# A two-layer backbone in one kernel: another order of block products in the first MLP, one chain for the plain blocks, and modulation rows in another place

## The chip, the cores and the metric

The kernel runs on one core of one Trainium2 chip, as one program. The metric is the device time of one execution in microseconds; the median of several executions counts. A core has TensorE (PE, the matmuls), VectorE (DVE), ScalarE (ACT), GpSimd (POOL) and SyncE (SP), which here only issues DMA loads. ACT and POOL issue the stores. Each engine works through its own instructions in order and waits for others by semaphores. Matmul results lie in PSUM until another engine moves them out.

## What is computed

Two layers over 1024 latent and 256 context tokens of width 1024. Each has a modulated in-projection, a mix of differential attention, a short convolution and a Fourier transform, an out-projection with gated residual and layer norm, and an MLP with squared ReLU and again gated residual and norm:

```python
for l in range(DEPTH):                                  # 2
    mod_x = (silu_c @ w_mod[l] + b_mod[l])[:, None, :]  # six rows of 1024; the same for the context
    sh1, sc1, g1, sh2, sc2, g2 = jnp.split(mod_x, 6, axis=-1)
    px = modulate(x, sh1, sc1) @ w_in[l]                # x*(1+scale) + shift; also for ctx
    ...                                                 # attention, convolution, Fourier mix -> mix_x
    x = layer_norm(DEEPNORM_ALPHA * x + g1 * mix_x, ln1_g[l], ln1_b[l])
    x = layer_norm(DEEPNORM_ALPHA * x
                   + g2 * (jnp.square(jax.nn.relu(modulate(x, sh2, sc2) @ w_up[l])) @ w_down[l]),
                   ln2_g[l], ln2_b[l])
    if not last: ...                                    # the same two steps for ctx with its own gates
return x
```

Everything is float32. The first layer's MLP works on 1280 tokens (ten tiles of 128), the second layer's end on 1024.

## The kernel before

Each float32 product is made of three matmuls: an operand x is split into hi (a cast on ACT) and lo = x − hi (line 230, on DVE or POOL), and `mm3` issues hi·hi, hi·lo and lo·hi (lines 234 to 236). So each weight and each activation needs an ACT cast and a lo before PE can use it.

**First MLP, up.** The 32 hidden blocks of 128 are 4 plain ones (`plain`, whole products) and 14 pairs (p = 2 to 15). A pair is computed as a 2x2 block product with seven products rather than eight, `mlp_blocks0`. They are named 1, 5, 6, 2, 7, 3, 4; each has 24 matmuls of 320 columns. Products 1, 2 and 5 open a PSUM tile, 6, 7 and 4 go on in that of 1, and 3 in that of 5. So between 6, 7 and 4 the tile's value is copied out, and after 7 DVE reads the tile of 5 too (line 1931) before 3 may go on in it. The list `seq` sets the order of products over pairs, and for product n the work of the other engines is written out behind it: evacuation of n, hi of n+3, lo of n+2, weight sums of n+4, and the step `back` of the background work. `wload(p + 2)` at product 3 loads the weights of the next pair but one.

**First MLP, down.** `down_blocks` is a generator that the up part starts early with `next(down)`. It makes 7 groups of 35 products (6 matmuls of 512 columns each), with operands formed by `form`. Its 8 PSUM tiles are added into ten token tiles `acc[t]` by `evac` (line 2217). The table `tail` loads what comes next during the last products. Then the plain loop multiplies two plain blocks per token tile, adds them, multiplies the tile by the gate on POOL (line 2158, `fold_late`), and adds the residual on DVE (line 2161). `wm` converts weights; for the last tiles they are multiplied with the gate on POOL first (line 2172).

**Finish.** `finish_steps` does the other two plain blocks (`down(t)`, add in line 2397, statistics in 2398 to 2405), the norm (`fin`), the transposes for the next in-projection (`turn`, line 2413), and the first parts of that in-projection (`part`). Line 2405 is a power of −1/2 on POOL, and line 2381 a small product on DVE that needs it; the helper `stats` has the same pair in lines 1267 and 1269.

**In-projection and modulation.** The modulation rows of the second layer are computed on DVE in the background, since each is a vector times a matrix. `mod_jobs` makes 16 jobs per row, each with a load of 256 KB and accumulations (lines 337 and 339), and each four jobs end in a `mod_tail` with small matmuls on PE (lines 383 or 386) and a small DVE step (lines 392 or 399). `in_steps` runs them between its units and works off the rest at its end, before it starts the second V projection (`vproj`, evacuated in lines 604 and 606). `REST` numbers the rows: 6 is gate one of the second layer, 7 its gate two, 8 and 9 shift and scale two. `mlp_blocks` is the second layer's MLP with a similar order of products.

## Time and profile before

| what | value |
| --- | --- |
| median of three executions | 3020.53 us (3015.72 to 3021.08) |
| the profiled execution | 3015.05 us, of it the span 3013.3 us |
| PE busy | 2749.9 us, 91% |
| DVE, ACT, POOL busy | 2068.2, 1153.4, 1127.3 us |
| mean granted clock of TensorE | 0.96 |
| DMA | 469.21 MB, mean 156 GB/s |

The span is the profiled execution from its first to its last instruction, and the rest of its time lies around it. Times in rows count from the span's start. Where the granted clock is below 1.00, part of a stretch ran at 1.2 rather than 2.4 GHz, and PE's busy time there is longer for the same matmuls. A bracket in a timeline row is the time its engine was idle before, and the instruction that ended that. The stages lie in this order: first in-projection, attention and out-projection to about 780, plain blocks and pairs to 1220, down to 1578, plain loop and finish to 1683, second in-projection to 1940, attention and out-projection to 2390, second MLP up to 2650, down and the end to 3013.

### The profile page before, as it was taken

The numbers are of one execution on the slowest core, as the hardware profiler recorded it, in microseconds if no ns is written. First come the engines' busy times: TensorE is split into PE (matmuls) and PEld (weight loads), VectorE is DVE, ScalarE is ACT, GpSimd is POOL, SyncE is SP. The second block draws the span as 40 slices with busy tenths as digits, with TensorE's granted clock in tenths as the row PEclk, the third lists the DMA queues.
The fourth block names the chain that finished last, engine by engine and source line by source line (L and its number), as shares of the span: only waits on it lengthen the run. The fifth ranks groups of instructions, "written<-read, shape, count | busy, mean of one in ns | idle before, by whom it ended". The sixth has DMA issues, their size and how long they took to land. (4 is left out here: it accounts for less than half of the span.)

```text
span 3013.3 us, 37703 instructions
## 1 busy us (share of the span) xinstructions
PE 2749.9 (91%) x14290; PEld 2349.5 (78%) x14290; DVE 2068.2 (69%) x2926; ACT 1153.4 (38%) x1610; POOL 1127.3 (37%) x642
## 2 busy tenths in 40 slices
PE   7889999899889999899996999779989899999996
PEld 5788888778789999787784888668777778878875
DVE  6668778844557777578877565647845577568887
ACT  4221256524434344433321531126623455554331
POOL 3412145623100000465647710126756000048785
PEclk8999999999999999899998999889999999999998
DMA  6244652346545554534351344643346555464442
GB/s 255 81 165 130 199 129 52 121 161 229 192 160 206 173 171 153 215 127 147 121 190 59 112 147 158 201 123 88 112 152 190 180 187 199 154 237 151 150 161 91
DMA packets 229033, 469.21 MB, mean 156 GB/s; under 512 B 18958, under 2 KB 116724, under 8 KB 228852
## 3 DMA queue, kind: packets, MB, share of 16 engines
q1 hardware_dynamic: 208680, 395.43, 40.6%
q10 hardware_dynamic: 17292, 61.93, 5.3%
q0 software_dynamic: 2880, 9.44, 0.8%
q8 instruction: 113, 1.85, 0.2%
q14 instruction: 68, 0.56, 0.1%
HBM read 323.41 MB, written 143.31 MB: 155 GB/s over the span
## 5 line engine op out<-in xcount | busy, mean ns | idle before, releaser
L234 PE MATMUL q<-a,a 128*128 128x512 f32 (+1 forms) x1632 | 599.0, 367 | 53.8 <-DVE t L1931 26.7
L236 PE MATMUL q<-a,a 128*128 128x512 f32 (+2 forms) x1682 | 611.5, 364 | 3.2 <-DVE a L230 3.2
L235 PE MATMUL q<-a,a 128*128 128x512 f32 (+1 forms) x1618 | 591.7, 366 | 5.5 <-POOL a L230 5.5
L235 PE MATMUL p<-a,b 128*128 128x512 f32 (+1 forms) x1088 | 407.1, 374 | 1.1 <-POOL a L230 1.0
L234 PEld LDWEIGHTS q<-a,a 128*128 128x128 f32 x1632 | 311.2, 191 | 107.0 <-DVE t L1931 30.5
L230 POOL TENSOR_TENSOR a<-b,a 128x256 fp32r<-128x256 f32 (+2 forms) x163 | 249.2, 1539 | 331.8 <-ACT a L2081 156.4
L236 PEld LDWEIGHTS q<-a,a 128*128 128x128 f32 x1682 | 320.4, 190 | 47.0 <-DVE a L230 4.7
L235 PEld LDWEIGHTS q<-a,a 128*128 128x128 f32 x1618 | 309.0, 191 | 48.4 <-POOL a L230 6.7
L2217 DVE TENSOR_TENSOR b<-q,b 128x512 f32<-128x512 f32 x425 | 279.2, 684 | 95.7 <-PE q L236 95.2
L230 DVE TENSOR_TENSOR a<-a,a 128x1280 fp32r<-128x1280 f32 (+4 forms) x156 | 290.1, 1860 | 43.2 <-ACT a L2078 31.8
L234 PE MATMUL p<-a,b 128*128 128x512 f32 (+1 forms) x816 | 305.2, 374 | 7.5 <-ACT b L1833 3.6
L236 PE MATMUL p<-a,b 128*128 128x512 f32 (+1 forms) x800 | 293.1, 366 | 3.9 <-DVE b L230 3.9
L234 PE MATMUL q<-b,a 128*128 128x256 f32 (+1 forms) x740 | 255.9, 346 | 41.0 <-DVE b L2217 15.8
L230 POOL TENSOR_TENSOR a<-a,a 128x1024 fp32r<-128x1024 f32 (+2 forms) x49 | 134.0, 2737 | 399.6 <-ACT a L2081 330.5
L339 DVE SCALAR_TENSOR_TENSOR m<-w,k,m 128x256 f32<-128x256 f32 x448 | 228.8, 523 | 48.1 <-DMA w<-wmr 38.8
L236 PE MATMUL q<-b,a 128*128 128x256 f32 (+1 forms) x740 | 252.6, 341 | 0.6 <-DVE a L230 0.6
L235 PE MATMUL q<-b,a 128*128 128x256 f32 (+1 forms) x740 | 252.7, 342 | 0.0
L235 PEld LDWEIGHTS p<-a,b 128*128 128x128 f32 x1088 | 208.2, 191 | 33.9 <-POOL a L230 1.9
L958 DVE TENSOR_REDUCE c<-p 128x1 f32<-128x1280 f32 x128 | 190.6, 1489 | 64.1 <-PE p L956 62.9
L989 ACT ACTIVATE a<-p,c 128x1280 f32<-128x1280 f32 x128 | 170.5, 1332 | 90.0 <-DVE c L958 82.6
L234 PEld LDWEIGHTS q<-b,a 128*128 128x128 f32 x740 | 144.7, 196 | 64.4 <-DVE b L2397 14.6
L234 PEld LDWEIGHTS p<-a,b 128*128 128x128 f32 x816 | 156.2, 191 | 34.3 <-issue 4.7
(300 smaller groups left out, 5412.6 us busy)
## 6 DMA issues: line engine op xcount, KB each, us to landing
a<-d SPq DMA_DIRECT2D x88, 512.0 KB
w<-wmr SPq DMA_DIRECT2D x160, 256.0 KB
a<-d SPq DMA_DIRECT2D x56, 640.0 KB
b<-wu SPq DMA_DIRECT2D x64, 512.0 KB
d<-t SPq DMA_DIRECT2D x46, 640.0 KB
b<-wd SPq DMA_DIRECT2D x54, 512.0 KB
d<-a ACTq DMA_DIRECT2D x40, 640.0 KB
a<-d SPq DMA_DIRECT2D x80, 320.0 KB
```

The source lines that it names most:

```text
L230: (eng or self.nc.vector).tensor_tensor(out, x, hi, op=ALU.subtract)
L234: mm(out, lh, rh, start=start, stop=False, skip_group_check=on)
L235: mm(out, lh, rl, start=False, stop=False, skip_group_check=on)
L236: mm(out, ll, rh, start=False, stop=stop, skip_group_check=on)
L339: nc.vector.scalar_tensor_tensor(a, w[:, i], s, a, op0=ALU.mult, op1=ALU.add)
L958: nc.vector.reduce_max(mx, ps[:, :nkey], axis=AX.X, negate=True)
L989: self.nc.scalar.activation(e[:, :nkey], ps[:, :nkey], AF.Exp, bias=mx, accum_out=s)
L2217: v.tensor_tensor(a, ps, a, op=ALU.add)
```

## The change

1. `in_steps`: the second layer's rows are 6, 8 and 9 rather than 6 to 9. Row 7 is computed in the second layer's MLP, which gets `tail` steps at products 7 and 3, and a `back` step at product 2 too.
2. `stats`: −mean on DVE first, then the power and the product on POOL. `finish_last` and the finish use it.
3. `mlp_blocks0`: another `seq`, the first two weights converted within the last plain block, and `wload(p + 2)` earlier in the step of product 3.
4. `down_blocks` in the first layer: the lo of the first group's weights on DVE, a further `yield`, evacuation after one product, and all four plain weights and activations loaded and converted in `tail`. The plain loop, `fold_late` and the scaling of weights are gone.
5. `finish_steps`: one chain over all four plain blocks per token tile and half (`half`), then `gate` on POOL, `resid` on DVE one tile later, and `norm`. The weights of the in-projection are loaded and converted at t = 8 and after rather than from t = 0.

```diff
@@ in_steps
-        for i in range(NREST0) if l == 0 else range(NREST1, len(REST)):
+        for i in (6, 8, 9) if l else range(NREST0):
@@ stats
+        m = self.sm([128, 1], bufs=12)
+        nc.vector.tensor_scalar(m, mv[:, 0:1], -1.0, None, op0=ALU.mult)
         nc.gpsimd.tensor_tensor(r, r, self.mhalf[:, 0:1], op=ALU.pow)
-        nc.vector.scalar_tensor_tensor(m, mv[:, 0:1], -1.0, r, op0=ALU.mult, op1=ALU.mult)
+        nc.gpsimd.tensor_tensor(m, m, r, op=ALU.mult)
@@ mlp_blocks
-        bg = self.stream(self.resid_jobs(l, T))
+        bg = self.stream(self.resid_jobs(l, T) + self.mod_jobs(7))
-            if i in (5, 6, 4, 3):
+            if i in (5, 6, 2, 4, 3):
                 back()
+            if i in (7, 3):
+                tail()
@@ mlp_blocks0
-        seq = [(NPL, 1), (NPL, 2)]
-        for p in range(NPL, NP):
-            seq += [(p, 5), (p, 6)] + [(p, 2)] * (p > NPL) + [(p, 7), (p, 3)]
-            seq += [(p + 1, 1)] * (p < NP - 1) + [(p, 4)]
+        a, b = NPL, NPL + 1
+        seq = [(a, 1), (a, 2), (b, 1), (a, 5), (a, 6), (b, 2), (a, 7), (a, 3), (a, 4)]
+        seq += [(b, 5), (b, 6), (b + 1, 1), (b, 7), (b, 3), (b, 4)]
+        for p in range(b + 1, NP):
+            seq += [(p, 5), (p, 6), (p, 2), (p, 7)] + [(p + 1, 1)] * (p < NP - 1) + [(p, 3), (p, 4)]
...
-        st.append(plain(3, {0: [P(sum_add, 3)], 1: [P(sum_split, 3), st[2], P(wload, NPL + 1)], 2: [back], 3: [back],
-                            4: [back], 5: [back]}))
+        st.append(plain(3, {0: [P(sum_add, 3)], 1: [P(sum_split, 3), P(wload, NPL + 1), P(wsum, 0), P(wsum, 1)],
+                            2: [lambda: st[2](), back], 3: [back], 4: [P(whi, 0), P(wlo, 0)], 5: [P(whi, 1), P(wlo, 1)]}))
...
+            if i == 3:
+                wload(p + 2)
             wsum(k + 4)
...
-            if i == 3:
-                wload(p + 2)
...
-            if p == NP - 1 and i in (2, 7, 3):
+            if p == NP - 1 and i in (6, 2, 7, 3, 4):
                 next(down)
@@ down_blocks
-            self.lo(wl, x, wh, g)
+            self.lo(wl, x, wh, g if n or l else v)
+        if l == 0:
+            yield
...
-            tail = {-16: P(wl, 0), -13: P(wl, 1), -12: P(wm, False), -10: P(hraw, 0), -9: P(wm, False), -8: P(hraw, 1),
-                    -7: hconv, -6: gload, -5: hconv, -4: P(gload, 1), -3: P(rload, 0), -2: P(rload, 1)}
+            tail = {-20: P(wl, 0), -18: P(wl, 1), -16: whi, -15: wlo, -14: P(wl, 2), -13: whi, -12: wlo,
+                    -11: P(hraw, 0), -10: whi, -9: wlo, -8: hconv, -7: P(hraw, 1), -6: P(wl, 3), -5: hconv,
+                    -4: [P(hraw, 2), P(hraw, 3)], -3: [gload, P(rload, 0)], -2: hconv, -1: whi}
+        lag = 2 if l else 1
-            evac(2, ps)
+            evac(lag, ps)
...
-        for t in range(T):                     # the plain loop: 6 matmuls per tile and half,
-            ...                                # an add each, fold_late(t), the tasks of tile t
+        wlo()
+        hconv()
+        self.gs[1] = self.bcast(self.grow[(l, 5, 1)])
@@ finish_steps
+        def half(t, c):
+            ps = self.p1()
+            sl = slice(128 * t, 128 * t + 128)
+            for i in range(4):
+                self.mm3(ps, H[i][0][:, sl], H[i][1][:, sl], W[i][0][:, c:c + 512], W[i][1][:, c:c + 512], i == 0, i == 3)
+            y = self.acc[t][:, c:c + 512]
+            nc.vector.tensor_tensor(y, ps, y, op=ALU.add)
+        def gate(t):
+            nc.gpsimd.tensor_tensor(y, y, self.gs[int(t >= 8)], op=ALU.mult)
+        def resid(t):
+            nc.vector.scalar_tensor_tensor(y, xr.pop(t)[:, :D], ALPHA, y, op0=ALU.mult, op1=ALU.add)
+        def norm(t):                           # bn_stats of both halves, stats(), Identity on ACT, store
+        def down(t):
+            half(t, 0);   resid(t - 1)
+            half(t, 512); norm(t - 1)
+            gate(t);      rload(t + 1)
```

PE, at the join of products 7 and 3 in the middle of the pairs: before, the last matmul of 7 and the first of 3, then the joins to (p+1, 1) and to 4. `q_1323` is the tile of product 1, `q_1332` that of 5, `q_1347` that of the next pair.

```order
L236 MATMUL q_1323_8121<-t_1232_6797,a_1025_5530 128x320
L234 MATMUL q_1332_8201<-a_1026_5531,a_1018_5523 128x320
...
L236 MATMUL q_1332_8201<-a_1032_5537,a_1019_5524 128x320
L234 MATMUL q_1347_8390<-a_1018_5523,a_1020_5525 128x320
...
L236 MATMUL q_1347_8390<-a_1024_5529,a_1021_5526 128x320
L234 MATMUL q_1323_8121<-a_1203_6652,a_1022_5527 128x320
```

```order
L236 MATMUL q_1322_8091<-t_1232_6807,a_1025_5532 128x320
L234 MATMUL q_1344_8356<-a_1018_5525 128x320
...
L236 MATMUL q_1344_8356<-a_1024_5531,a_1019_5526 128x320
L234 MATMUL q_1331_8205<-a_1026_5533,a_1020_5527 128x320
...
L236 MATMUL q_1331_8205<-a_1032_5539,a_1021_5528 128x320
L234 MATMUL q_1322_8091<-a_1203_6662,a_1022_5529 128x320
```

Product 3 (`q_1332`, now `q_1331`) stood right behind 7 and now stands behind product 1 of the next pair (`q_1344`).

POOL, in the plain loop before and in the finish after: `b` are the token tiles, line 2158 and after it line 2382 the gate, 1269 and 1270 power and product, `c` columns of 128.

```order
L2172 TENSOR_TENSOR a_1814_12865<-a_1814_12865,a_1807_12799 128x1024
L2158 TENSOR_TENSOR b_1527_10585<-b_1527_10585,a_1807_12799 128x1024
L230 TENSOR_TENSOR a_1825_12950<-a_1819_12906,a_1824_12949 128x1280
L2158 TENSOR_TENSOR b_1529_10595<-b_1529_10595,a_1807_12799 128x1024
L2172 TENSOR_TENSOR a_1815_12882<-a_1815_12882,a_1807_12799 128x1024
L2158 TENSOR_TENSOR b_1533_10608<-b_1533_10608,a_1807_12799 128x1024
L2158 TENSOR_TENSOR b_1536_10620<-b_1536_10620,a_1807_12799 128x1024
```

```order
L2382 TENSOR_TENSOR b_1521_10559<-b_1521_10559,a_1817_12849 128x1024
L1269 TENSOR_TENSOR c_1836_12962<-c_1836_12962,k_5_75 128x1
L1270 TENSOR_TENSOR c_1837_12964<-c_1837_12964,c_1836_12962 128x1
L2382 TENSOR_TENSOR b_1524_10569<-b_1524_10569,a_1817_12849 128x1024
L1269 TENSOR_TENSOR c_1844_13008<-c_1844_13008,k_5_75 128x1
L1270 TENSOR_TENSOR c_1845_13010<-c_1845_13010,c_1844_13008 128x1
L2382 TENSOR_TENSOR b_1527_10581<-b_1527_10581,a_1817_12849 128x1024
```

Gates stood among weights' products and lo's of 1280 columns, ahead of all statistics; now power, product and gate alternate tile by tile.

DVE, in the finish at one token tile: before the add, statistics and the small product of line 2381 (of the tile before); after the add (2378), the residual (2386) and the statistics.

```order
L2397 TENSOR_TENSOR b_1525_10568<-q_1853_13129,b_1525_10568 128x512
L2398 BN_STATS c_1852_13128<-b_1525_10568 128x6
L2381 SCALAR_TENSOR_TENSOR c_1854_13138<-c_1849_13120,c_1850_13122 128x1
L2397 TENSOR_TENSOR b_1525_10568<-q_1856_13143,b_1525_10568 128x512
L2398 BN_STATS c_1852_13128<-b_1525_10568 128x6
L2402 BN_AGGR c_1857_13152<-c_1852_13128 128x2
L2404 TENSOR_SCALAR c_1858_13154<-c_1857_13152 128x1
```

```order
L2378 TENSOR_TENSOR b_1527_10581<-q_1840_12974,b_1527_10581 128x512
L2386 SCALAR_TENSOR_TENSOR b_1524_10569<-a_1831_12926,b_1524_10569 128x1024
L2378 TENSOR_TENSOR b_1527_10581<-q_1841_12989,b_1527_10581 128x512
L2392 BN_STATS c_1842_13003<-b_1524_10569 128x6 x2
L1264 BN_AGGR c_1843_13006<-c_1842_13003 128x2
L1266 TENSOR_SCALAR c_1844_13008<-c_1843_13006 128x1
L1268 TENSOR_SCALAR c_1845_13010<-c_1843_13006 128x1
```

The residual stands between the adds of the next tile, and the small product that read POOL's power is gone; line 1268 takes −mean from the aggregate alone.

DVE, from the end of the second in-projection to the first copy of the V projection (line 606): `m` are sums of modulation jobs.

```order
L230 TENSOR_TENSOR a_2257_15661<-a_2254_15653,a_2256_15660 128x1024
L399 SCALAR_TENSOR_TENSOR k_8_85<-q_2251_15645,k_9_86 128x2
L339 SCALAR_TENSOR_TENSOR m_2253_15650<-w_2252_15648,k_6_77,m_2253_15650 128x256 x2
L339 SCALAR_TENSOR_TENSOR m_2253_15650<-w_2260_15669,k_6_77,m_2253_15650 128x256 x2
L339 SCALAR_TENSOR_TENSOR m_2253_15650<-w_2261_15673,k_6_77,m_2253_15650 128x256 x2
L399 SCALAR_TENSOR_TENSOR k_8_85<-q_2262_15677,k_9_86 128x2
L337 TENSOR_SCALAR m_2265_15687<-w_2263_15680,k_6_77 128x256
L339 SCALAR_TENSOR_TENSOR m_2265_15687<-w_2263_15680,k_6_77,m_2265_15687 128x256
L339 SCALAR_TENSOR_TENSOR m_2265_15687<-w_2264_15685,k_6_77,m_2265_15687 128x256 x2
L339 SCALAR_TENSOR_TENSOR m_2265_15687<-w_2266_15690,k_6_77,m_2265_15687 128x256 x2
L339 SCALAR_TENSOR_TENSOR m_2265_15687<-w_2267_15694,k_6_77,m_2265_15687 128x256 x2
L399 SCALAR_TENSOR_TENSOR k_8_85<-q_2268_15698,k_9_86 128x2
```

```order
L566 STREAM_SHUFFLE b_2228_15531<-a_2220_15498 128x1024
L568 TENSOR_TENSOR b_2228_15531<-b_2228_15531,b_1982_13736 128x1024
L230 TENSOR_TENSOR b_2230_15536<-b_2214_15423,b_2229_15535 128x1024
L570 TENSOR_TENSOR a_2220_15498<-a_2220_15498,b_2228_15531 128x1024
L230 TENSOR_TENSOR b_2235_15558<-b_2231_15539,b_2234_15557 128x1024
L230 TENSOR_TENSOR a_2233_15555<-a_2220_15498,a_2232_15554 128x1280
L566 STREAM_SHUFFLE b_2239_15592<-a_2238_15590 128x1024
L568 TENSOR_TENSOR b_2239_15592<-b_2239_15592,b_1982_13736 128x1024
L570 TENSOR_TENSOR a_2238_15590<-a_2238_15590,b_2239_15592 128x1024
```

Jobs and tails stood between the last unit's work and the V projection; now the last unit's work (lines 566 to 570), lo's of V's weights and of a key or query stand there.

## Rows read from the trace of the kernel before

**Rows 1.** Page, section 1: busy us (share), instructions.
```profile
PE 2749.9 (91%) x14290; PEld 2349.5 (78%) x14290; DVE 2068.2 (69%) x2926; ACT 1153.4 (38%) x1610; POOL 1127.3 (37%) x642
```

**Rows 2.** Windows by stage: start:end, length, busy us (instructions) by engine, clock, DMA share, GB/s.
```profile
850.00:1215.00 365.00, 339.18 (x2268) 332.58 (x2269) 267.05 (x507) 147.27 (x236) 8.11 (x15) 0.99 0.53 180
1578.00:1683.00 105.00, 75.87 (x311) 58.52 (x311) 78.78 (x109) 28.95 (x33) 70.20 (x38) 0.85 0.21 81
2390.00:2650.00 260.00, 257.16 (x1129) 211.29 (x1129) 173.31 (x303) 134.19 (x240) 8.75 (x16) 1.00 0.53 181
```

**Rows 3.** Timeline, a pair of the first MLP: start, us, engine, line, op, out<-in, [idle<-releaser].
```profile
1044.07 0.69 ACT L1929 COPY t<-q 128x640 f32<-128x640 f32 x1 [5.31 <-PE q L236]
...
1045.98 0.82 DVE L1931 TENSOR_TENSOR t<-q,t 128x640 f32<-128x640 f32 x1
...
1046.86 0.41 PE L234 MATMUL q<-a,a 128*128 128x320 f32 x1 [1.87 <-DVE t L1931]
```

**Rows 4.** Waits, 850 to 1215: engine, line<-releaser: us in total, times, longest.
```profile
PE q L234 <- DVE t L1931: 26.7, 14, 6.1
...
ACT t L1929 <- DMA d<-t: 9.8, 1, 9.8
```

**Rows 5.** Timeline of PE, entry to the pairs.
```profile
823.75 0.63 PE L234 MATMUL q<-a 128*128 128x320 f32 x1 [4.71 <-ACT a L1894]
...
827.69 0.63 PE L236 MATMUL q<-a,a 128*128 128x320 f32 x1 [3.04 <-DVE a L230]
```

**Rows 6.** Timeline of PE, start of down.
```profile
1224.30 0.80 PE L234 MATMUL q<-a,a 128*128 128x512 f32 x1 [2.96 <-ACT a L2081]
...
1228.11 0.80 PE L235 MATMUL q<-a,a 128*128 128x512 f32 x1 [3.01 <-POOL a L230]
...
1244.80 0.79 PE L234 MATMUL q<-a,a 128*128 128x512 f32 x1 [3.33 <-ACT b L2215]
```

**Rows 7.** Timeline of PE, plain loop and finish.
```profile
1577.83 0.39 PE L234 MATMUL q<-b,a 128*128 128x512 f32 x1
...
1622.95 0.77 PE L234 MATMUL q<-b,a 128*128 128x512 f32 x1 [13.71 <-DVE b L2217]
...
1682.64 0.55 PE L2413 MATMUL q<-k,b 128*128 128x128 f32 x3
```

**Rows 8.** Three lines: duration ns min/median/max, first and last start us, form.
```profile
L2158 POOL TENSOR_TENSOR b<-b,a x10: 2338/3273/3386, 1581.5 to 1627.7; 128x1024 f32<-128x1024 f32 x10
...
L2161 DVE SCALAR_TENSOR_TENSOR b<-a,b x10: 1212/2010/3357, 1586.8 to 1632.0; 128x1024 f32<-128x1024 f32 x10
...
L2405 POOL TENSOR_TENSOR c<-c,k x10: 537/542/1523, 1636.4 to 1678.3; 128x1 f32<-128x1 f32 x10
```

**Rows 9.** Groups by form, 1560 to 1690: busy us, mean ns | idle before, releaser.
```profile
L2217 DVE TENSOR_TENSOR b<-q,b 128x512 f32<-128x512 f32 x35 | 23.2, 685 | 8.9 <-PE q L236 8.9
...
L2398 DVE BATCH_NORM_STATS2 c<-b 128x6 f32<-128x512 f32 x20 | 13.9, 695 | 0.7
...
L2381 DVE SCALAR_TENSOR_TENSOR c<-c,c 128x1 f32<-128x1 f32 x10 | 10.3, 1032 | 0.4 <-POOL c L2405 0.4
...
L2402 DVE BATCH_NORM_AGGREGATE c<-c 128x2 f32<-128x12 f32 x10 | 2.1, 209 | 0.3
L2404 DVE TENSOR_SCALAR c<-c 128x1 f32<-128x1 f32 x10 | 1.5, 154 | 0.3
```

**Rows 10.** Timeline of PE, end of the second in-projection.
```profile
1958.66 0.98 PE L386 MATMUL q<-k,m 128*128 128x2 f32 x4 [17.75 <-DVE m L339]
1973.20 0.98 PE L386 MATMUL q<-k,m 128*128 128x2 f32 x4 [13.56 <-DVE k L399]
...
1981.69 0.56 PE L234 MATMUL q<-b,a 128*128 128x256 f32 x1
```

**Rows 11.** Timeline of ACT, there.
```profile
1952.97 1.04 ACT L2280 CAST b<-b 128x1024 fp32r<-128x1024 f32 x1 [10.02 <-DMA b<-wv]
```

**Rows 12.** Groups of DVE, 1930 to 1985.
```profile
L339 DVE SCALAR_TENSOR_TENSOR m<-w,k,m 128x256 f32<-128x256 f32 x23 | 11.1, 483 | 8.3 <-DMA w<-wmr 7.8
```

179 lines of the change are left out of this document (76 added, 103 removed).

## The prediction

> **What bounds the kernel now.** I read the page first: PE is busy 2749.9 of 3013.3 us [rows 1], so about 263 us can be won at most while the matmuls stay what they are, and they do: the two programs issue the same 13,027 PE instructions. Then I cut the span into the stages that the diff touches and asked the windows view what PE does in each [rows 2]. The pairs of the first MLP leave PE idle 365.00 − 339.18 = 25.8 us, plain blocks and finish 105.00 − 75.87 = 29.1, while the second layer's MLP leaves 2.8 and has nothing to give. Last I looked up in the list of waits and in the timelines who releases PE at the end of each long pause. The reader should see four kinds: fourteen short ones at one line [rows 3, 4], two starts of a stage where converted weights are missing [rows 5, 6], one long one in the plain loop [rows 7], and a drain of leftover jobs before the second attention [rows 10].
>
> **Part by part.**
>
> *The pairs of the first MLP.* Product 3 accumulates in the bank of product 5, and DVE's L1931 still has to read that bank when it adds 5 to 7. Before, product 3 stands right behind product 7: ACT copies 7 (0.69 us), DVE adds (0.82 us), and PE starts 0.06 us after DVE's end, 1.87 us late [rows 3]. In all 26.7 us in 14 times, longest 6.1 [rows 4]. Now (p+1, 1) stands between 7 and 3 in 11 of 14 pairs; it has its own bank. A product has 24 matmuls, so 365.00 / 2268 × 24 = 3.86 us cover the 1.87, with 2 us to spare. Without the longest, 13 waits average (26.7 − 6.1) / 13 = 1.58; 11 of them make 17.4. The last pair and the first two keep 7 beside 3. The 6.1 is pair two, where ACT also stood 9.8 us at an old store of the tile it writes [rows 4]; the rewoven start may keep that or lose it, so of 6.1 − 1.6 = 4.5 I take half, 2.2. Sum **19.6**, from 12 (DVE reaches L1931 late, as its queue of weight sums is unchanged while the pair is shorter) to 24. The load of pair p+2 moves ahead of DVE's later work in the same step, but its first use comes a product sooner; SP's queue keeps its order of loads and stores there. That cover is the third rival.
>
> *Entry to the pairs.* PE waits 4.71 us for ACT's cast and 3.04 us for DVE's remainder [rows 5]. Both now stand inside the last plain block. ACT must still empty that block's bank before its next work, so I keep the first wait and take the second: **3**, from 1 to 5. The store of plain block 2 moves behind one weight load on SP; nobody waits for it soon.
>
> *Start of down.* Three waits, 2.96 + 3.01 + 3.33 = 9.3 us: an ACT cast, POOL's remainder, an ACT copy queued behind casts that wait for a load [rows 6]. The first forms are now begun four products earlier and their remainders go to DVE. DVE gets the last pair's sums and about six remainders in one row there, so the third wait shrinks but stays. I take **6**, from 3 to 9. In the products of down, evacuations follow after one product rather than two: **1**, from 0 to 4.
>
> *Plain blocks, gate, residual, norm.* Before: from 1577.83 to 1682.64, where the transposes of the fourth column block begin, 104.8 us, with 13.71 us in one pause [rows 7]. 311 matmuls are busy 75.87 us there, 0.244 each [rows 2]. The merged chain cuts 20 DVE adds, and no weight waits any more for POOL's gate multiplication. What is late next is a loop through the engines: gate(t) on POOL stands behind pow and product of tile t−1, these wait for DVE's statistics, these for the residual, and that for gate(t−1). One turn: residual 1.21 and gate 2.34 at their shortest, pow 0.54 in the median [rows 8]; add 0.685, two bn_stats 1.39, aggregate 0.21, two small ones 0.31 [rows 9]. The new POOL product has no row; its like in size is pow, so between 0 and 0.54, and I take 0.54. Sum 7.23 us, against 24 × 0.244 = 5.9 of matmuls: the loop bounds the stage, PE waits about 1.4 per tile. Gate(0) ends at 5.9 + 0.7 + 2.3 = 8.9 after the products; gate(8) starts at 8.9 + 8 × 7.23 − 2.34 = 64.4; two more turns (14.5) and the last normalisation with the casts behind it (about 6.5, an estimate from ACT's order) bring the same transposes at 85.4. In four tiles POOL also makes remainders for the transposed blocks beside the residual. Where POOL works beside it, the residual takes 2.01 in the median [rows 8], 4 × 0.8 = 3.2. So 88.6 in place of 104.8: **16**. Ends: with gate at 3.27 and residual at 2.01 in every tile, a turn is 8.96 and the gain about 3; with PE alone as the bound, 29.
>
> The residual spreads from 1.21 to 3.36 us and the gate from 2.34 to 3.39 [rows 8]. The Trainium skill, page "SBUF — State Buffer", section "Who interferes with whom", has a rule that speaks against this loop: a DVE instruction with two SBUF inputs and a GpSimd instruction that reads SBUF shut each other out, and the second waits the whole time. The spread agrees with it. By that rule I would charge the four tiles the longest residual, 4 × (3.36 − 1.21) = 8.6, and the term would be 10.6 and the forecast 2956.
>
> *Statistics elsewhere.* DVE's small product (mean 1.03 us [rows 9]) was short in itself and long because it waited in DVE's queue for POOL. Now ACT waits for POOL directly; behind it on ACT stand evacuations. **1**, from 0 to 4.
>
> *Modulation rows.* After the last in-projection matmul PE only meets tails of jobs: 17.75 and 13.56 idle, a third shorter one, and the V projection starts at 1981.69 [rows 10]. DVE does 23 accumulations of 0.48 us after 1930, waiting 7.8 for their loads [rows 12]: some twelve jobs left. Sixteen are taken away, so none should be left. What is late next is the second half of V's weights: ACT waited 10.02 for its load and cast it from 1952.97 for 1.04 [rows 11], DVE's remainder adds about 1.2, 1955.2. 1981.69 − 1955.2 = **26**. Ends: 36 if the load comes as much sooner as ACT waited, 16 if the keys' work, now beside the V projection instead of in the drain, holds DVE another 10.
>
> In the second layer's MLP the sixteen jobs cost DVE 32 × 0.483 = 15.5 us, with 16 loads, 4 small stores and 4 tails on PE. DVE is busy 173.31 of 260 there and PE 257.16 [rows 2]. So between 0 and 15.5, and as DVE has 86 us free, near the low end: **−3**, to −10.
>
> **The sum.** 19.6 + 3 + 6 + 1 + 16 + 1 + 26 − 3 = 69.6. The profiled execution took 3015.05 us (its span 3013.3), which gives 2945; it ran 5.5 below the median 3020.53 of the three runs, so I forecast **2951** for the median. All low ends at once give about 2995 and all high ends about 2910.
>
> **Rivals.** *Short loop gains* (chance 0.22): the loop through POOL turns at 8.96, gain 3 rather than 16, and the V weights come no sooner than DVE allows, 16 rather than 26. For it: residual and gate already lengthen each other [rows 8]. Against: in the new loop they follow each other by their data. 2951 + 13 + 10 = 2974.
>
> *The joins don't vanish* (0.08): the change doesn't do there what it says, because DVE comes to L1931 more than 2 us later than now and PE meets it one product on. Its queue is busy 267.05 of 365.00 [rows 2], which speaks against. 2951 + 17 = 2968.
>
> *Weights late in the pairs* (0.06), the slower side: pair p+2's weights have a product less from load to use, behind modulation loads and stores on SP. Every pair then pauses as pair two did, 6.1 [rows 4]: 14 × 6.1 = 85.4 against 26.7 today, a loss of 58.7 where 19.6 were booked: 2951 + 19.6 + 58.7 = 3029. It decides from a loss of 50 / 14 = 3.6 us per pair on; only one pair in 14 shows such a pause today.
>
> *PE-bound finish and early V weights* (0.14): 29 and 36 in place of 16 and 26: 2928.
>
> **Chances.** The forecast, from 2938 to 2963, has 0.45; 0.05 is left for what I don't see. A measurement of this kernel tells about 0.2% from no change, 6 us. Slower by more: 0.06 and a little of the unseen, 0.07. Within: 0.03. Faster: 0.90. The range 2920 to 2986 holds the forecast, both smaller gains and the larger one, and leaves out the late weights and the ends of the rest.
>
> **What would show it.** Pairs: L1931's total as PE's releaser falls from 26.7 to between 5 and 10, and a pair gets shorter by 1.6. Entry and down: the 3.04 and 3.01 are gone. Plain and finish: one chain per tile every 7 to 8 us, PE released by the adds, and POOL nearly without idle. Drain: no tail of jobs between the in-projection and V, one wait of some 13 us for a weight. Second MLP: PE idle under 6 us. I'm wrong if weights release PE in the pairs, if a turn of the loop exceeds 9, or if V still starts 30 us after the last in-projection matmul.

## The result: 2948 us, a ratio of 0.9765, and where 71 us went

| | before | after |
| --- | --- | --- |
| median, same chip | 3018.21 us (3015.72 to 3021.08) | 2948.0 us (2943.8 to 2949.78) |
| ratio, 95% interval | | 0.9765 (0.9748 to 0.9782) |
| profiled execution, its span | 3015.05, 3013.3 us | 2943.8, 2941.9 us |

The forecast was 2951 from 2920 to 2986: the time lies 3 us from it, by a sum in which gains and losses that I had sized wrongly cancel. Of gains, 69.6 us were forecast and 70.2 lie between the medians; that they come so close is luck. A table by stage shows it. Each boundary is the start of the same matmul in both timelines of PE; gains are in us of the profiled executions.

| stage | before | after | gain | forecast |
| --- | --- | --- | --- | --- |
| entry (its waits), then pairs to their end | 1221.34 | 1206.65 | 14.7 | 3 + 19.6 |
| start of down and down, to its last product | 1577.83 | 1551.78 | 11.4 | 6 + 1 |
| plain blocks, finish, in-projection to its last matmul | 1940.18 | 1895.56 | 18.6 | 16 |
| drain, second attention, to the second MLP | 2388.30 | 2309.50 | 34.2 | 26 |
| second MLP and its down to the last tiles | 2926.86 | 2849.28 | −1.2 | −3 |
| last tiles, to the end of the span | 3013.3 | 2941.9 | −6.2 | 1 |

The columns "before" and "after" give the time at which the stage ends; the end of the pairs is the first matmul of down, less the wait of 2.96 in front of it before [rows 6]. Code that is the same in two kernels differs by up to 5 us per stage between their profiled executions. The pairs, from the entry to the first matmul of down, took 384.2 here and 383.8 to 387.9 in six kernels below whose pairs are untouched; the stretch from the plain blocks to the last in-projection matmul took 343.8 here and 340.6 to 345.5 in seven. So smaller differences of a stage are not read from its length, but from its waits.

First the page's PE line of the changed kernel, then its windows over the pairs, plain blocks and finish, and the second MLP, columns as in [rows 2]:

```profile
PE 2743.8 (93%) x14290; PEld 2347.7 (80%) x14290; DVE 2015.1 (68%) x2915; ACT 1149.9 (39%) x1608; POOL 1099.0 (37%) x664
```

```profile
849.00:1206.65 357.65, 338.90 (x2282) 332.54 (x2280) 269.38 (x510) 148.93 (x238) 8.12 (x15) 0.99 0.55 188
1552.00:1635.90 83.90, 72.49 (x312) 56.71 (x311) 49.50 (x89) 23.96 (x27) 42.55 (x39) 0.92 0.34 121
2311.20:2571.20 260.00, 257.90 (x1130) 210.43 (x1130) 187.00 (x338) 133.10 (x237) 8.76 (x16) 1.00 0.58 196
```

PE's idle time in the span falls from 263.4 to 198.1; the other 6.1 of the 71.4 us are busy time of the same matmuls, at a mean clock of 0.97 rather than 0.96. In the pairs idle time falls from 25.8 to 18.8, between the products and the fourth column block from 29.1 to 11.4 for 312 instructions where there were 311. In the second MLP it stays near 2 (2.8 before), although DVE does 13.7 us more there: the moved row is hidden.

**Pairs.** A join in the timelines of ACT, PE and DVE of the changed kernel: product 7 is copied, product 1 of the next pair starts, and the add of line 1952 (1931 before) runs beside it.

```profile
1063.78 0.69 ACT L1950 COPY t<-q 128x640 f32<-128x640 f32 x1 [5.35 <-issue]
...
1064.34 0.39 PE L234 MATMUL q<-a,a 128*128 128x320 f32 x1
...
1065.46 0.82 DVE L1952 TENSOR_TENSOR t<-q,t 128x640 f32<-128x640 f32 x1
```

PE no longer waits for the add at 1065.46, as it did at 1046.86 in [rows 3]. But its other releasers, absent before (the list of waits, 850 to 1200), are now there:

```profile
PE q L234 <- DVE t L1952: 10.0, 3, 6.6
...
PE q L236 <- DVE a L230: 5.0, 5, 1.5
...
PE q L234 <- DVE c L392: 2.1, 1, 2.1
...
PE q L234 <- DVE k L399: 1.7, 1, 1.7
```

14 joins of 26.7 us are 3 of 10.0, and 8.8 us of new waits stand against it: remainders that DVE delivers late now that a pair is shorter, and the opening product's bank that a tail of a modulation job still holds. The 6.6 is pair two's, as before [rows 4], but not for the store: ACT copies the tile at 874.51 and waits for no store. The add stands on DVE behind a background job that waits for its load (first row), 2.3 us ahead of PE's row (second).

```profile
878.85 0.43 DVE L1498 TENSOR_TENSOR w<-w,m 128x256 f32<-128x256 f32 x1 [6.20 <-DMA w<-d]
...
881.13 0.63 PE L234 MATMUL q<-a,a 128*128 128x320 f32 x1 [6.65 <-DVE t L1952]
```

**Entry and down.** The two waits of the entry [rows 5] are 3.93 and 1.23. At the start of down the three of [rows 6] are two, PE's rows first; then DVE's and POOL's beside the first:

```profile
1214.62 0.47 PE L234 MATMUL q<-a,a 128*128 128x512 f32 x1 [3.60 <-DVE k L399]
1226.07 0.80 PE L234 MATMUL q<-a,a 128*128 128x512 f32 x1 [2.78 <-ACT b L2235]
...
1209.33 5.00 DVE L230 TENSOR_TENSOR a<-a,a 128x1280 fp32r<-128x1280 f32 x2 [2.31 <-ACT a L2095]
...
1209.66 3.59 POOL L2086 TENSOR_TENSOR a<-a,a 128x1024 f32<-128x1024 f32 x1
```

The last tail's small step (line 399) stands in DVE's queue behind two remainders that take 5.00 us beside POOL; without POOL two take 2.62 (at 1203.26, where POOL is idle).

The larger part of this stage's gain lies behind its start. By the start of the same matmul, the first 240 of down's 1470 matmuls are 4.9 us shorter and the other 1230 are 6.4 us shorter. There PE waited nine times for DVE's evacuation of a bank, and now once, since the evacuation follows after one product rather than two. PE's waits, before (1250 to 1578) and after (1235 to 1552):

```profile
PE q L234 <- DVE b L2217: 5.2, 9, 1.0
...
PE q L234 <- DVE b L2237: 1.3, 1, 1.3
```

**Finish.** One turn of the loop on POOL, timeline:

```profile
1572.02 0.55 POOL L1269 TENSOR_TENSOR c<-c,k 128x1 f32<-128x1 f32 x1 [3.56 <-DVE c L1268]
1572.64 0.19 POOL L1270 TENSOR_TENSOR c<-c,c 128x1 f32<-128x1 f32 x1
1572.78 2.39 POOL L2382 TENSOR_TENSOR b<-b,a 128x1024 f32<-128x1024 f32 x1
1578.74 0.54 POOL L1269 TENSOR_TENSOR c<-c,k 128x1 f32<-128x1 f32 x1 [3.56 <-DVE c L1268]
```

1578.74 − 1572.02 = 6.72 us per tile (6.70 to 6.78 in seven turns), where 7.23 was forecast. The transposes of the fourth column block, at 1682.64 in [rows 7], begin at 1635.57, 83.8 after the products rather than 104.8; 85.4 with every residual at its shortest, and 88.6 with four longer ones, were forecast. Of these 21.0 us the rest of the in-projection gives back 2.4. Its weights now come at tile 8, and PE waits for their cast 4.12 us in the first place:

```profile
1617.92 0.50 PE L234 MATMUL p<-a,b 128*128 128x512 f32 x1 [4.12 <-ACT b L2290]
...
1635.57 0.60 PE L2417 MATMUL q<-k,b 128*128 128x128 f32 x4
```

**Drain.** PE's timeline from the last in-projection matmul to the V projection, against [rows 10]:

```profile
1895.56 0.39 PE L236 MATMUL p<-a,b 128*128 128x512 f32 x1
1895.78 0.50 PE L386 MATMUL q<-k,m 128*128 128x2 f32 x4
1896.14 0.37 PE L234 MATMUL q<-b,a 128*128 128x256 f32 x1
...
1900.44 0.38 PE L234 MATMUL q<-b,a 128*128 128x256 f32 x1 [2.62 <-ACT b L2290]
```

41.5 us became 0.6. A wait of 2.62 for V's second weights and one of 0.87 follow, in place of the 10.02 that ACT alone waited in [rows 11]; it waits 4.57 now:

```profile
1899.35 1.04 ACT L2290 CAST b<-b 128x1024 fp32r<-128x1024 f32 x1 [4.57 <-DMA b<-wv]
```

SP issues that load at 1891.33, 4.2 us ahead of the last in-projection matmul, and before at 1942.19, 2.0 behind it. With these waits in it, the stretch from V's first matmul to the second MLP takes 413.4 rather than 406.6 (408.3 to 415.0 in the kernels below that have the row in the second MLP), so of 40.9 there remain 34.2.

**End.** Here 6.2 us are lost, and 4.9 in six kernels below with the same end (91.4 us, where the kernel before has 86.4). The residual of line 2153 (2172 after), once per source view of each kernel, before first (durations in ns: min/median/max), then the timeline of DVE and POOL after:

```profile
L2153 DVE SCALAR_TENSOR_TENSOR b<-a,b x8: 1207/1226/3407, 2936.4 to 2981.8; 128x1024 f32<-128x1024 f32 x8
```

```profile
L2172 DVE SCALAR_TENSOR_TENSOR b<-a,b x8: 1210/3396/3406, 2858.8 to 2907.6; 128x1024 f32<-128x1024 f32 x8
...
2886.97 3.40 DVE L2172 SCALAR_TENSOR_TENSOR b<-a,b 128x1024 f32<-128x1024 f32 x1 [3.22 <-POOL b L2171]
...
2886.91 2.39 POOL L2318 TENSOR_TENSOR b<-b,b 128x1024 f32<-128x1024 f32 x1
```

The new statistics release ACT, and by it POOL's product with the norm's gain (line 2318), so early that it starts with DVE's next residual: POOL takes its 2.39 and DVE 1.23 + 2.2.

### The profile page after: what moved, and what is told of

The parts are those of the page before. It is cut to its first block, busy times and chain, and to the rows that moved or that the text cites. A ratio compares the mean times of both kernels' runs of the same rounds, so it can differ in the third digit from the quotient of the medians.

```text
span 2941.9 us, 37767 instructions
## 1 busy us (share of the span) xinstructions
PE 2743.8 (93%) x14290; PEld 2347.7 (80%) x14290; DVE 2015.1 (68%) x2915; ACT 1149.9 (39%) x1608; POOL 1099.0 (37%) x664
## 3 DMA queue, kind: packets, MB, share of 16 engines
q1 hardware_dynamic: 208392, 394.39, 41.5%
## 4 chain that ended last, share of the span: by engine, by line
PE 68%; DVE 11%; issue 6%; POOL 5%; DMA 5%; ACT 4%; SPq 1%; ACTq 0%; DVEq 0%; POOLq 0%
PE q L234 14%; PE q L236 14%; PE q L235 14%; PE p L234 5%; PE p L236 5%; PE p L235 5%; PE q L1025 3%; PE p L955 2%; PE p L956 2%; PE q L1012 2%; DVE c L958 2%; DVE a L230 1%; POOL a L230 1%; DVE b L230 1%; DMA d<-a 1%
## 5 line engine op out<-in xcount | busy, mean ns | idle before, releaser
L234 PE MATMUL q<-a,a 128*128 128x512 f32 (+1 forms) x1610 | 587.9, 365 | 34.9 <-DVE b L2237 13.7
L236 PE MATMUL q<-a,a 128*128 128x512 f32 (+2 forms) x1658 | 601.2, 363 | 5.0 <-DVE a L230 5.0
L235 PE MATMUL q<-a,a 128*128 128x512 f32 (+1 forms) x1594 | 581.6, 365 | 3.2 <-POOL a L230 3.2
L234 PEld LDWEIGHTS q<-a,a 128*128 128x128 f32 x1610 | 305.2, 190 | 82.7 <-DVE t L1952 10.8
L236 PEld LDWEIGHTS q<-a,a 128*128 128x128 f32 x1658 | 314.2, 190 | 49.6 <-DVE a L230 7.4
L230 POOL TENSOR_TENSOR a<-b,a 128x256 fp32r<-128x256 f32 (+1 forms) x137 | 220.1, 1614 | 345.1 <-ACT a L2098 193.6
L2237 DVE TENSOR_TENSOR b<-q,b 128x512 f32<-128x512 f32 x405 | 268.7, 684 | 110.8 <-PE q L236 109.7
L235 PEld LDWEIGHTS q<-a,a 128*128 128x128 f32 x1594 | 302.4, 190 | 45.3 <-POOL a L230 4.3
L230 DVE TENSOR_TENSOR a<-a,a 128x1024 fp32r<-128x1024 f32 (+4 forms) x163 | 266.7, 1639 | 38.3 <-ACT a L2095 27.5
L234 PE MATMUL q<-b,a 128*128 128x256 f32 (+1 forms) x748 | 256.7, 343 | 18.6 <-ACT b L604 8.4
L235 PEld LDWEIGHTS p<-a,b 128*128 128x128 f32 x1088 | 209.3, 192 | 34.2 <-POOL a L230 1.9
L234 PEld LDWEIGHTS p<-a,b 128*128 128x128 f32 x816 | 157.5, 193 | 39.3 <-ACT b L2290 9.3
L236 PEld LDWEIGHTS p<-a,b 128*128 128x128 f32 x800 | 153.9, 192 | 32.2 <-DVE b L230 7.0
L234 PEld LDWEIGHTS q<-b,a 128*128 128x128 f32 x748 | 144.8, 194 | 41.0 <-ACT b L604 11.4
```

The source lines that it names most:

```text
L230: (eng or self.nc.vector).tensor_tensor(out, x, hi, op=ALU.subtract)
L234: mm(out, lh, rh, start=start, stop=False, skip_group_check=on)
L235: mm(out, lh, rl, start=False, stop=False, skip_group_check=on)
L236: mm(out, ll, rh, start=False, stop=stop, skip_group_check=on)
L2237: v.tensor_tensor(a, ps, a, op=ALU.add)
```

## Experiments

Line numbers shift by up to 10 between these kernels; times are medians, ratios to the kernel before with 95% intervals. The kernel before, timed beside each, has medians from 3016.9 to 3021.0 us, so differences between the medians of two of these kernels are sure to a few us only; where the ratios say something else, both are given.

**Is the drain the moved row?** The changed kernel with row 7 back in the in-projection.

```diff
-        for i in (6, 8, 9) if l else range(NREST0):
+        for i in (6, 7, 8, 9) if l else range(NREST0):
-        bg = self.stream(self.resid_jobs(l, T) + self.mod_jobs(7))
+        bg = self.stream(self.resid_jobs(l, T))
...
-            if i in (5, 6, 2, 4, 3):
+            if i in (5, 6, 4, 3):
                 back()
-            if i in (7, 3):
-                tail()
```

> The changed kernel with the modulation rows put back: row 7 is computed in the second in-projection again, and not in the second MLP. Theory (the drain's leftover jobs hold PE): PE meets tails of jobs again between the last in-projection matmul and the V projection, some 35 us of it, since V started 4.7 us after that matmul in the changed kernel and 41 us in the kernel before; the second MLP gets about 1 us shorter. So about 2948 + 35 = 2983 us. Rival (the stage's gain came from the in-projection starting otherwise, and V's weights would have been late anyway): V starts less than 20 us after the last matmul, 2948 + 10 = 2958 us.

Measured: 2985.26 us, 0.9889 (0.9874 to 0.9905). Waits of PE, 1900 to 1960:

```profile
PE q L386 <- DVE k L399: 20.4, 2, 13.6
PE q L386 <- DVE m L339: 18.1, 1, 18.1
```

The drain is back, 42.05 us against 41.5 before. SP issues V's second load at 1910.92 here, 2.5 us behind the last in-projection matmul, as before. Part 1 alone is worth 37.3 us, over half of the whole. Its price in the second MLP is too small to read: from its start to the last tiles 541.4 us without the row, and 539.8 with it.

**What is the order of products worth?** The old list `seq`, all else as changed.

```diff
-        seq = [(a, 1), (a, 2), (b, 1), (a, 5), (a, 6), (b, 2), (a, 7), (a, 3), (a, 4)]
-        seq += [(b, 5), (b, 6), (b + 1, 1), (b, 7), (b, 3), (b, 4)]
...
+        seq = [(NPL, 1), (NPL, 2)]
+        for p in range(NPL, NP):
+            seq += [(p, 5), (p, 6)] + [(p, 2)] * (p > NPL) + [(p, 7), (p, 3)]
+            seq += [(p + 1, 1)] * (p < NP - 1) + [(p, 4)]
```

> The changed kernel with the old order of products over the pairs of the first MLP; all else stays. Theory (the wait at the join of 7 and 3 is the order's): the wait for the line that adds 5 to 7 returns in all 14 pairs, 10.0 to about 26 us, while the new waits of PE in that stage (for remainders, and for tails of modulation jobs, 8.8 us in all) go, since they follow from the tighter order; net 8 to 13 us longer, 2956 to 2961 us. Rival (the new waits are not the order's): they stay, and the time rises by the whole 16 us, 2964 us.

Measured: 2956.0 us, 0.9791 (0.9777 to 0.9806), 8.0 above the changed kernel. Waits of PE, 850 to 1212, two lines in all:

```profile
PE q L234 <- DVE t L1951: 20.0, 12, 2.4
PE q L236 <- DVE a L230: 1.8, 1, 1.8
```

The joins return, with one more of 1.64 at 1213.21, and the new waits go but for one. They come to 21.6 us in 13 rather than the expected 26 in 14: pair two's pause is 2.4 here, since in this order the job that waits for its load stands behind the add. The stage takes 397.7 us from the entry, 10 to 14 more than with the new order. The order is worth about 8 us net, where the forecast took 17.4 for eleven joins; the two intervals overlap slightly, so that the size is rough.

**Do the new waits in the pairs cost what they show?** Two small edits, each alone: the tails of modulation jobs at product 2 rather than 7, so that no tail stands in front of an opening product; and no background step behind the first product of pair two.

```diff
-            if i == 7:
+            if i == 2:
                 tail()
```

> The changed kernel with the step of the modulation tails in the first MLP's pairs at product 2 rather than at product 7. In the changed kernel product 1 of the next pair opens a bank right behind product 7, and twice waits for DVE to read a tail out of it (2.07 and 1.73 us). Theory: with the tail read a product earlier these two waits go, and nothing else changes: 2944 us. Rival (the bank isn't the reason, DVE's queue is): the waits only move to another product, 2948 us.

```diff
-            back(BKU[i])
+            if (p, i) != (b + 1, 1):
+                back(BKU[i])
```

> The changed kernel without the one background step at product 1 of the fourth hidden pair's place (the step right before the seventh product of pair two). In the changed kernel pair two still pauses 6.65 us at its join, with DVE standing 6.20 us at a background job's load ahead of the addition that PE waits for. Theory (DVE's queue order holds the addition): the pause falls to about 1.6 and the eleven matmuls at half clock behind it go too, 2948 - 6 = 2942 us. Rival (the pause is ACT's or the store's, as in the kernel before, where ACT waited 9.8 us for a store): it stays above 4 us, 2948 us.

Measured: 2942.82 us, 0.9752 (0.9735 to 0.977), and 2941.03, 0.9745 (0.973 to 0.9759), against 0.9765 (0.9748 to 0.9782) for the changed kernel. PE's waits in the pairs, first the tail edit (to 1240), then the skipped step (to 1200):

```profile
PE q L234 <- DVE k L399: 6.3, 1, 6.3
...
PE q L383 <- DVE t L1955: 0.9, 1, 0.9
PE q L386 <- DVE t L1955: 0.9, 1, 0.9
```

```profile
PE q L234 <- DVE t L1952: 4.2, 3, 1.6
```

Each wait goes where it was aimed at (L392 is gone in the first, pair two's 6.6 is 1.6 in the second). At the start of down line 399 now holds PE 6.3 and 6.4 us, but in place of two waits, 3.60 and 2.78, and down takes 345.6 and 345.2 us as in the changed kernel (345.1): nothing is lost there. The medians lie 5.2 and 7.0 us under the changed kernel's, but the intervals overlap: what each edit is worth is not settled by these runs.

**What is the start of down worth?** The first group's weight remainders back on POOL and evacuation after two products.

```diff
-            self.lo(wl, x, wh, g if n or l else v)
+            self.lo(wl, x, wh, g)
...
-        lag = 2 if l else 1
+        lag = 2
```

> The changed kernel with two parts of the start of the down part undone: remainders of the first weights on POOL again, and evacuation after two products rather than one. Theory (these two parts bring a part of the stage's gain, 4 us of about 6): the start of down pauses longer on POOL's remainders, 2952 us. Rival (the gain there comes from beginning the first forms earlier, and DVE's remainders, which take up to 3.5 us beside POOL, cost as much as they bring): 2946 to 2949 us.

Measured: 2957.74 us, 0.9806 (0.9789 to 0.9822), 9.7 above by the medians and 12 by the ratios. At the start of down PE stands once, at 1236.01, and behind it the nine waits of before are back (PE, 1205 to 1260, then 1240 to 1569):

```profile
PE q L234 <- ACT b L2235: 12.2, 1, 12.2
...
PE q L234 <- DVE b L2237: 5.2, 9, 1.0
```

From its first matmul to its end down takes 356.9 rather than 345.1, 5.3 of it in the first 240 matmuls and 6.5 behind them. These two edits bring 10 to 12 us where 6 + 1 were booked, more than half of it in the loop that was booked at 1. Which of the two brings the start's part is not separated.

**Is the loss at the end a collision of DVE and POOL?** The old statistics in the last tiles only; then the changed kernel with POOL's product of line 2318 replaced by a fill, which leaves the norm's gain out of the result.

```diff
@@ finish_last
+            nc.vector.scalar_tensor_tensor(m, mean, -1.0, r, op0=ALU.mult, op1=ALU.mult)
             nc.scalar.activation(y, y, AF.Identity, bias=m, scale=r)
...
-            st[t] = r, _, mean = self.stats(s6)
...
+            nc.vector.bn_aggr(mv, s6)
...
+            nc.gpsimd.tensor_tensor(r, r, self.mhalf[:, 0:1], op=ALU.pow)
```

> The changed kernel with the old statistics at the very end (the last tiles of the second layer): the small product of mean and power on DVE, one tile later, rather than on POOL at once. In the changed kernel three residual additions on DVE take 3.40 us each rather than 1.23, beside a POOL product that starts at the same time. Theory (the two engines exclude each other, and the old place of the small product keeps them apart): the residuals are back at 1.23, the end of the kernel is 6 us shorter, 2942 us. Rival (the end is longer for POOL's two small instructions per tile, 0.2 us each, or for the stores): residuals stay at 3.40 or the time changes by under 2 us, 2946 to 2948 us.

```diff
-            nc.gpsimd.tensor_tensor(o[t], y, lg, op=ALU.mult)
+            nc.gpsimd.memset(o[t], 0.5)
```

> The changed kernel, with POOL's product by the norm's scale in the last tiles replaced by a fill of the same tile with a constant, which reads nothing from SBUF; this product is left out, so the output isn't the reference's. Theory (two engines exclude each other where both read SBUF): the three residuals of 3.40 us are back at about 1.2 although POOL still works at the same moment, and the end of the kernel is some 6 us shorter. Rival (POOL's writes or its mere activity slow DVE): they stay above 3.

Measured: 2939.72 us, 0.974 (0.9723 to 0.9757), the last tiles 86.5 us as before (86.4) rather than 92.6; and 2944.16 in one run, the last tiles 82.3. The residual with the old statistics, then a tile of the fill kernel, POOL and DVE:

```profile
L2172 DVE SCALAR_TENSOR_TENSOR b<-a,b x8: 1208/1226/3400, 2859.3 to 2904.6; 128x1024 f32<-128x1024 f32 x8
```

```profile
2896.25 0.95 POOL L2318 MEMSET b<- 128x1024 f32 x1
...
2896.35 1.23 DVE L2172 SCALAR_TENSOR_TENSOR b<-a,b 128x1024 f32<-128x1024 f32 x1 [3.23 <-POOL b L2171]
```

With the old statistics ACT waits for DVE's small product, POOL's product starts 4.06 us after the end of its gate and meets no residual. With the fill POOL is as early as in the changed kernel, 0.85 of its 0.95 us lie beside the residual, and DVE isn't held at all: the cause is an operation that reads, not a busy POOL. The Trainium skill, page "SBUF — State Buffer", section "Who interferes with whom", says that a DVE instruction with two SBUF inputs contends with a GpSimd instruction that reads SBUF, and not with one that only writes it; these rows agree, 3.40 us beside the product and 1.23 beside the fill.

**And elsewhere?** The old statistics everywhere, in `stats` too.

```diff
+        nc.gpsimd.tensor_tensor(r, r, self.mhalf[:, 0:1], op=ALU.pow)
         m = self.sm([128, 1], bufs=12)
-        nc.vector.tensor_scalar(m, mv[:, 0:1], -1.0, None, op0=ALU.mult)
-        nc.gpsimd.tensor_tensor(r, r, self.mhalf[:, 0:1], op=ALU.pow)
-        nc.gpsimd.tensor_tensor(m, m, r, op=ALU.mult)
+        nc.vector.scalar_tensor_tensor(m, mv[:, 0:1], -1.0, r, op0=ALU.mult, op1=ALU.mult)
```

> The changed kernel with the old statistics everywhere: the small product of mean and power on DVE again, in the helper and in the last tiles. The last tiles alone gave 2939.7 us. Theory (elsewhere the new place of the product brings almost nothing): 2938 to 2942 us. Rival (in the finish's loop and in the out-projections DVE's wait for POOL costs as it did before, one to two us per tile): 2950 us or more.

Measured: 2952.73 us, 0.9772 (0.9757 to 0.9786), above the kernel with the old statistics in the last tiles only by 13.0 in the medians and by 9.7 in the ratios: the rival came true. Its timeline of DVE and POOL in the finish:

```profile
1572.37 2.34 DVE L1269 SCALAR_TENSOR_TENSOR c<-c,c 128x1 f32<-128x1 f32 x1 [0.66 <-POOL c L1267]
...
1572.32 2.38 POOL L2389 TENSOR_TENSOR b<-b,a 128x1024 f32<-128x1024 f32 x1
```

A product of 128 numbers, with two inputs in SBUF, takes 2.34 us where POOL's gate has started 0.05 us before it; the same operation takes 0.16 in the median of the whole program. A turn is 6.96 us at first and 8.6 beside the transposes (gates at 1601.85, 1610.45, 1619.02), where the changed kernel has 6.77. The windows of PE from 1601 to 1651, changed kernel first, this one second:

```profile
1601.00:1651.00 50.00, 40.51 (x174) 30.75 (x173) 23.36 (x39) 22.10 (x32) 30.67 (x28) 0.86 0.29 95
```

```profile
1601.00:1651.00 50.00, 34.18 (x127) 25.73 (x126) 30.97 (x38) 18.59 (x24) 24.94 (x20) 0.76 0.28 95
```

PE issues 47 matmuls fewer there, and its granted clock is 0.76 on average rather than 0.86, so more of the stretch runs at 1.2 GHz. The stage to the last in-projection matmul takes 356.1 rather than 343.8. The same edit thus gains about 12 us in the finish and loses 5 to 6 at the end. In the out-projections it shows nothing: the pairs' entry comes at 822.58 here and at 822.49 in the changed kernel, and from V to the second MLP it is 412.9 and 413.4 us.

**Is the loop through POOL the bound of the finish?** If so, taking the norm of tile t−1 out of the gate's way must shorten a turn. First in all tiles of the changed kernel:

```diff
+            if t < T:
+                gate(t)
             if t:
                 norm(t - 1)
             if t < T:
-                gate(t)
                 rload(t + 1)
```

> The changed kernel with one swap in the first layer's finish: the gate of tile t stands on POOL ahead of power and product of tile t-1, rather than behind. Theory (a loop through POOL and DVE bounds the finish, 6.72 us per tile in the changed kernel's trace): the loop is cut, each tile costs PE's 24 matmuls, 5.5 us, so over eight or nine tiles 9 to 11 us are won, less what the in-projection's weights, loaded at a fixed tile, then make PE wait longer: 2938 to 2942 us. Rival (PE or DVE's own work is the bound, and the loop only follows): tiles stay at 6.5 or more, 2947 us.

Measured: 2946.06 us, 0.9757 (0.9741 to 0.9773). POOL's gates in the first tiles, then beside the transposes; and PE's wait there:

```profile
1568.64 2.40 POOL L2382 TENSOR_TENSOR b<-b,a 128x1024 f32<-128x1024 f32 x1 [3.04 <-DVE b L2378]
1574.09 2.40 POOL L2382 TENSOR_TENSOR b<-b,a 128x1024 f32<-128x1024 f32 x1 [1.62 <-DVE b L2378]
...
1599.27 2.41 POOL L2382 TENSOR_TENSOR b<-b,a 128x1024 f32<-128x1024 f32 x1
...
1606.20 2.54 POOL L230 TENSOR_TENSOR a<-w,a 128x512 fp32r<-128x512 f32 x2 [3.21 <-ACT a L2430]
1608.70 2.38 POOL L2382 TENSOR_TENSOR b<-b,a 128x1024 f32<-128x1024 f32 x1
```

```profile
1625.79 0.79 PE L234 MATMUL p<-a,b 128*128 128x512 f32 x1 [9.77 <-ACT b L2290]
```

5.45 us per tile in the first five turns, and POOL now waits for PE's chain: the loop was the bound. But from the sixth on a turn is 8.9 to 9.4, since there the remainders of the transposed blocks stand in POOL's queue ahead of the gate and wait for ACT themselves (fourth row), and the weights' cast stands on ACT behind that work. The stage takes 344.4, as in the changed kernel (343.8), and the time is the rival's, not the expected 2938 to 2942.

**A better version.** The old statistics in the last tiles, the tails at 2, the skipped step, and the last tails flushed before down's second operands; then gate first in all tiles and three loads more before those operands; then gate first in six tiles only.

```diff
-            if p == NP - 1 and i in (6, 2, 7, 3, 4):
+            if p == NP - 1 and i in (6, 2, 7, 3):
                 next(down)
...
         while tails:
             tail()
+        next(down)
...
-        loads_to(7 if l else 6)
+        loads_to(7 if l else 9)
...
+            if t < 6:
+                gate(t)
             if t:
                 norm(t - 1)
             if t < T:
-                gate(t)
+                if t >= 6:
+                    gate(t)
                 rload(t + 1)
```

> The changed kernel with four corrections at once: the old statistics in the last tiles, modulation tails at product 2, no background step before the join of pair two, and the last tails flushed ahead of the down part's second operands, so that DVE reads the tail's bank before it makes the remainders of down. If the four terms are independent: 6 + 4 + 6 + 3 = 19 us less than 2948, 2929 us. Rival (what is won in the pairs is lost again at the start of down, where loads set the pace): 2938 us.

> The four corrections of the run before (last tiles, tails, background step, flush) with the swapped gate, and three more loads of the down part issued ahead of the last pair's store. Theory: the pause of 7.1 us for ACT's copy at the start of down, behind casts that wait for loads, falls to 3 or less, and the gate's swap adds its own gain: 2937 - 4 - 9 = 2924 us. Rival (the loads wait for tiles that the last products still read, and the pause stays): 2928 us.

> The best version so far, with the gate of tile t ahead of the norm of tile t-1 on POOL in the first six tiles only; from tile 6 on, where the transposes' remainders also stand on POOL, the order is that of the changed kernel. Theory (the later tiles' order lost what the first six gained): turns of 5.4 us in tiles 0 to 5 and of 6.7 to 8 after, the stage from the end of the products to the last matmul of the in-projection falls from 348.7 to 338 to 341 us, and the whole comes to 2924 to 2929. Rival (the weights of the in-projection, converted behind their load at tile 8, bound the stage whatever the first tiles do): the wait of PE for the cast in line 2292 stays at 8 us or more, the stage at 344 to 349, the whole at 2932 to 2939.

Measured: 2937.12 us, 0.9733 (0.9718 to 0.9747); 2934.72, 0.9711 (0.9697 to 0.9725); 2931.47, 0.9704 (0.9682 to 0.9727). The first missed its expected 2929 and came to the rival's 2938: at the start of down PE waits 7.1 us for ACT's copy of line 2237. In the second that wait is 3.5. The second missed its expected 2924 to 2928, because gate first in all tiles gives nothing. The third kept the short turns and lost the long ones: its ninth gate starts 56.9 us after the products, against 61.2 in the second and 61.5 in the changed kernel, and PE's wait for the cast is 2.96 (here a row of PE).

```profile
1609.70 0.80 PE L234 MATMUL p<-a,b 128*128 128x512 f32 x1 [2.96 <-ACT b L2292]
```

The stage from the end of the products to the last in-projection matmul takes 339.5, against 348.7 in the second and 343.8 in the changed kernel; but two kernels with the old place of the gate have 340.6, so the turns show the theory, and the stage's length alone doesn't. The whole came out 2.5 us above its expected range. It has the lowest median of all, 16.5 us below the changed kernel, with an interval that overlaps the second's.

## Why the prediction was right, and where its steps were wrong

*Failed: statistics elsewhere (+1, measured −5 to −6 at the end).* The step read the old small product's mean of 1.03 us [rows 9] as short work waiting in DVE's queue. The mean mixes two kinds, as the source view of the kernel before shows:

```profile
L2381 DVE SCALAR_TENSOR_TENSOR c<-c,c x10: 142/640/2259, 1638.2 to 1679.8; 128x1 f32<-128x1 f32 x10
```

Five of the ten took 1.12 to 2.26 us, each begun while a POOL operation on 128x1024 of 2.35 to 2.38 us ran, and five, with POOL idle, took 0.14 to 0.16. It was the collision, not the queue. And the step asked only who waits for the moved product, not what POOL and ACT start sooner by it; the sooner product of line 2318 then shuts out a residual of 1.23 us for 2.2.

*Mis-sized: drain (26, measured 34.2, high end 36).* The mechanism held: no tail of jobs, then a wait for a V weight. But the waits are 2.62 + 0.87 rather than 13, since the load is issued ahead of the stage's end, not behind it as before; with the row's jobs put back it is issued behind it again. The prediction had an earlier load as its high end and took none.

*Mis-sized: pairs (19.6, measured about 12 here, and about 8 by the executions in which the same pairs took 387.9).* The joins fell as forecast, 26.7 to 10.0. Not booked were 8.8 us of other waits: product 1 opens a bank that a tail still uses, and DVE is late with weights' remainders. Pair two's 6.1 was left at half and stayed whole; the store that the prediction named no longer holds ACT, and a background job's load on DVE takes its place. So the term came out at its low end of 12 or under it. The entry held, 2.6 for 3.

*Mis-sized: start of down (6, measured 4.9) and its loop (1 from 0 to 4, measured 6.4).* At the start two waits of 6.4 us stand in place of three of 9.3, and the third did stay, 2.78 for 3.33. The term that failed is the loop: the 1 came from no row, while PE's list of waits held nine waits of 5.2 us for the evacuation there. One of 1.3 is left, and with evacuation after two products all nine are back.

*Held: plain blocks and finish (16, measured 21.0 to the transposes it was reckoned to, 18.6 to the last in-projection matmul).* The loop bounds it, and a turn is 6.72. Of the 0.51 us between that and 7.23, the second POOL product is 0.35 (0.19 for the 0.54 assumed); two bn_stats at 1.28 for 1.39 give another 0.11. The residual is 1.23 us at the longest in all ten tiles, since by their data it begins when a gate has ended, and POOL then waits 0.86 to 3.56 us for others. So POOL is not "nearly without idle" as the signs had it. The charge of 8.6 by the Trainium skill's rule didn't arise here, and arose where no one looked, at the end.

*Held: second MLP (−3, measured −1.2, which the stage's length can't tell from 0).* DVE's 86 idle us took it, as its 187.00 us busy in the window and PE's idle time of 2.1 show.

Both programs issue the same number of PE instructions, as the bound wants; the traces count 14290 in each, where the prediction gives 13,027.

The rivals: weights released PE five times in the pairs, so that sign of being wrong did show, but with 1.5 us at the longest, where 6.1 in every pair was feared; three joins of 14 were left, not all; a turn was not 8.96. The one nearest was the larger gain in the drain, without its PE-bound finish.

## What to carry to other kernels

When small steps of a chain go from one engine to another, ask for each of the two what it now starts sooner, and lay that beside the DVE instructions of the same moment that read two inputs from SBUF; the same edit gained about 12 us in one loop and lost 5 to 6 in another. Where a mean is far above the size of the work, look at the single instructions: 1.03 us was half at 0.15 and half at up to 2.26. Give no term a size without its row: nine short waits of 5.2 us in all stood in the list, and the term was put at 1. A wait that is covered returns in part as waits of others once the stage is shorter: book the net, which was half here. And look for background work that is left over in front of a stage: moving one row of it to a stage with an idle DVE brought over half of all that was gained.

## What the runs showed of the hardware

POOL holds up DVE by what it reads, not by being busy: beside a product of 2.39 us a residual of 1.23 took 3.40, beside a fill of 0.95 it took 1.23. A DVE add of 128x512 with one input in PSUM, wholly within a gate (the kernel with gate first, at 1600.05), took 0.69, as long as elsewhere. Size is no protection: a DVE product of 128x1 took 2.34 us beside POOL's gate and 0.16 in the median, 15 times as long. Two remainders of 128x1280 took 5.00 us beside POOL and 2.62 without it. A POOL product of 128x1 takes 0.19 us and its power 0.54, so that moving such a small step to POOL costs less than one collision.
